# Gate products of a hybrid decoder layer in seven block products for eight

## The chip, the cores and the metric

The kernel runs on one core of a Trainium2 chip. The metric is the device time of one execution in microseconds (us); the median over the runs shown is what a change is measured by. The five engines are named as in the profile: PE (matrix products; PEld is its loading of weights), DVE (vector), ACT (scalar), POOL (GpSimd) and SP (which only issues transfers here).

## What is computed

One layer on 512 tokens of width 2048, float32. Only the part around the change is shown; the attention-like branch (`gated_delta_rule`), the pooling branch, the mixture of experts and the last gate lie before and behind it.

```python
n1 = rms_norm(h, norm_mix[i])                       # (512, 2048)
proj = n1 @ w_in[i]                                 # u_pool 1024, q, k, v, z 4096, b, a, then
u_pool, qkv, z, b_lin, a_lin, gate_pool, gate_dn = split_columns(proj)   # two gates of 2048
...
merged = (jax.nn.sigmoid(gate_pool) * (y_pool @ w_up_pool[i])
          + jax.nn.sigmoid(gate_dn) * (y_dn @ w_up_dn[i]))
h = h + merged @ w_out[i]
```

## The kernel before

Everything is held transposed: a tile has 128 channels on its partitions and the 512 tokens along the free axis. `n1h[k]`, `n1l[k]` (k = 0 to 15) hold the normed input as a rounded part and the rest, so that a float32 product is made of three products in the faster format, `mm3` (L99 to L103): high weights by high input, high weights by low input, low weights by high input. Each of the three is one matmul of 128x128 weights by 128x512 input.

Weights come in chunks of 128x1024 (`raw`, 512 KB): four k-tiles of 256 output columns. `load_w` (L324) has SP fetch a chunk and splits it: ACT rounds it into `whi` (L96), DVE subtracts to get `wlo` (L97, two inputs in SBUF, the on-chip memory of the engines). `next_w` hands out one chunk and starts the split of the next, so a split runs beside the matmuls of the chunk before it; `whi` and `wlo` have two buffers, `raw` three.

`proj` (L375) makes 256 output columns in two PSUM banks (PSUM is where PE accumulates): 24 matmuls for each chunk, four chunks for a gate (2048 channels in), two for an up-projection (1024 in). After the delta branch, whose last head ends at the start of this stage, `merge_dn` and `merge_pool` take eight column pairs each. For every pair `gate_up` makes the gate's product, ACT writes `sg` = tanh of half of it (a sigmoid is taken as (tanh + 1)/2), and then the up-projection's product is made from `ydh`, `ydl` or `yph`, `ypl`. DVE multiplies the two (L474, L486). In the first pair stands `pool_mix`, which needs the eight tiles `d` that `load_diffs` fetches from DRAM. The order of work on each engine here is that of a scheduler over the program's order.

Pools of SBUF are opened and closed like a stack, on a left and a right side; a tile in reused space waits until its predecessors there are done.

Of the kernel before, what the change touches and what calls it, by code (L numbers as in the profile page):

```python
# [21 lines left out]
KD = D // P  # L22
# [15 lines left out]
C_GP = 5136  # L38
C_GD = 7184
# [25 lines left out]
class Layer:  # L65
# [162 lines left out]
    def norm_in(self, sources):  # L228
        nc, px = self.nc, self.px
# [3 lines left out]
        self.rs = px.tile([P, NT], F32, name="rs", bufs=1)  # L233
        raw = []
        for _ in range(4):
            src, width = next(sources)
# [27 lines left out]
        ps = [self.bank("mm"), self.bank("mm")]  # L264
# [56 lines left out]
            self.xs.append(x)  # L321


    def load_w(self, src, width):  # L324
        nc = self.nc
        raw = self.p_w.tile([P, 1024], F32, name="raw", bufs=3)
        hi = self.p_w.tile([P, 1024], F32R, name="whi", bufs=2)
        lo = self.p_w.tile([P, 1024], F32R, name="wlo", bufs=2)
        r = raw.rearrange("p (k c) -> p k c", c=width)
        nc.sync.dma_start(r, src)  # L330
        self.last_split = self.split(hi, lo, raw)
        return hi.rearrange("p (k c) -> p k c", c=width), lo.rearrange("p (k c) -> p k c", c=width)

    def mixer_sources(self):
        a, w = self.a, self.a["w_in"][0]

        def cols(m, c0):
            for k0 in range(0, m.shape[0], 4 * P):
                yield m[k0:k0 + 4 * P, c0:c0 + 256].rearrange("(k p) c -> p k c", p=P), 256
# [4 lines left out]
        for c0, up in ((C_GD, a["w_up_dn"][0]), (C_GP, a["w_up_pool"][0])):  # L344
            for cp in range(8):
                yield from cols(w, c0 + cp * 256)
                yield from cols(up, cp * 256)
                if cp == 0 and c0 == C_GD:
                    for g in (0, 2):
                        yield a["pool_w"][0, g:g + 2].rearrange("g (k p) c -> p (g k) c", p=P), 256  # L350
        for cb in range(4):
            for k0 in range(0, KD, 2):
                yield a["w_out"][0, k0 * P:(k0 + 2) * P, cb * T:(cb + 1) * T].rearrange("(k p) c -> p k c", p=P), T

    def start_weights(self, sources):
        self.pending, self.side = [], iter(())
        self.w_sources = sources
        self.w_next = self.load_w(*next(sources))

    def next_w(self):  # L360

        w = self.w_next
        src = next(self.w_sources, None)
        self.w_next = src and self.load_w(*src)
        return w

    @contextmanager
# [4 lines left out]
                s.enter_context(self.tc.issue_after(i.ins))  # L372
            yield

    def proj(self, xh, xl, tag="mm"):  # L375

        nk = len(xh)
        ps = [self.bank(tag), self.bank(tag)]
        for k0 in range(0, nk, 4):
            hi, lo = self.next_w()  # L380
            for k in range(4):
                for c in range(2):
                    s = slice(c * P, (c + 1) * P)
                    self.mm3(ps[c], hi[:, k, s], lo[:, k, s], xh[k0 + k], xl[k0 + k],
                             start=k0 + k == 0, stop=k0 + k == nk - 1)
                with self.behind(self.last_split):
                    self.tick()
                    if k in EXTRA:
                        self.tick()
        return ps  # L390

    def tick(self):
        if self.pending:
            self.pending.pop(0)()
        else:
            next(self.side, None)
# [56 lines left out]
                    self.yph.append(h)  # L453
                    self.ypl.append(l)

    def gate_up(self, pp, yh, yl):

        nc = self.nc
        ps = self.proj(self.n1h, self.n1l)
        sg = []  # L460
        for i in range(2):
            s = pp.tile([P, T], F32, name="sg", bufs=3)
            nc.scalar.activation(s, ps[i], AF.Tanh, scale=0.5)
            sg.append(s)
        return sg, self.proj(yh, yl)

    def merge_dn(self, pp):
        for cp in range(8):
            sg, ps = self.gate_up(pp, self.ydh, self.ydl)
            for i in range(2):  # L470
                n = 2 * cp + i
                if n >= 8:
                    self.md.append(self.p_md.tile([P, T], F32, name="md", tag=f"md{n}", bufs=1))
                self.nc.vector.scalar_tensor_tensor(self.md[n], sg[i], 1.0, ps[i], op0=OP.add, op1=OP.mult)  # L474
            if cp == 0:
                self.pool_mix()

    def merge_pool(self, pp):

        nc = self.nc  # L480
        self.m = []
        for cp in range(8):
            sg, ps = self.gate_up(pp, self.yph, self.ypl)
            for i in range(2):
                t = self.p_y.tile([P, T], F32, name="m", tag="yd", bufs=KD)
                nc.vector.scalar_tensor_tensor(t, sg[i], 1.0, ps[i], op0=OP.add, op1=OP.mult)  # L486
                nc.vector.tensor_tensor(t, t, self.md[2 * cp + i], op=OP.add)
                self.m.append(t)

# [1195 lines left out]
    def run(self):  # L1685
# [9 lines left out]
        self.p_dram = p_dram = self.ctx.enter_context(tc.tile_pool(name="saved", bufs=1, space=bass.MemoryType.DRAM))  # L1695
        self.h_dram = p_dram.tile([T, D], F32, name="h_dram")
        self.d_dram = p_dram.tile([8, P, T], F32, name="d_dram")
        self.p_n1, s_n1 = self.open("n1", "right")
        with tc.manual_schedule(engines={mybir.EngineType.Activation, mybir.EngineType.DVE, mybir.EngineType.PE}):
            self.norm_in(self.mixer_sources())  # L1700
# [6 lines left out]
        self.delta_branch(pd)  # L1707
        s_d.close()
        s_dc.close()
        self.p_md, s_md = self.open("md", "left")  # L1710
# [6 lines left out]
        s_n1.close()  # L1717
        s_yp.close()
        s_md.close()
        p_h, s_h = self.open("hp", "right")  # L1720
# [6 lines left out]
        pp, s_p = self.open("out_tmp", "left")  # L1727
# [13 lines left out]
        pp, s_p = self.open("router_tmp", "right")  # L1741
# [10 lines left out]
        pp, s_p = self.open("tail", "left")  # L1752
# [41 lines left out]
```

## Time and profile before

| | |
|---|---|
| time, median of 3 runs | 2546.79 us (2546.7 to 2548.34) |
| the profiled execution's own time | 2548.15 us |
| its span in the trace | 2546.4 us |
| mean granted clock of PE in it | 0.989 of full |

The profile is that of one execution; its span is shorter than its own time by 1.75 us, which lie around the first and the last instruction. Its rows are those of the sections below. A matmul's duration in them (389 ns for 512 columns) is that from its start to its end, and consecutive matmuls overlap: what PE delivers is read from the distance of their starts, in the timeline.

### The profile page before, as it was taken

The numbers are of one execution on the slowest core, as the hardware profiler recorded it, in microseconds if no ns is written. First come the engines' busy times: TensorE is split into PE (matmuls) and PEld (weight loads), VectorE is DVE, ScalarE is ACT, GpSimd is POOL, SyncE is SP. The second block draws the span as 40 slices with busy tenths as digits, with TensorE's granted clock in tenths as the row PEclk, the third lists the DMA queues.
The fourth block names the chain that finished last, engine by engine and source line by source line (L and its number), as shares of the span: only waits on it lengthen the run. The fifth ranks groups of instructions, "written<-read, shape, count | busy, mean of one in ns | idle before, by whom it ended". The sixth has DMA issues, their size and how long they took to land. (4 is left out here: it accounts for less than half of the span.)

```text
span 2546.4 us, 30523 instructions
## 1 busy us (share of the span) xinstructions
PE 2411.1 (95%) x11926; PEld 1652.8 (65%) x11926; DVE 1063.4 (42%) x1963; ACT 719.8 (28%) x1323; POOL 83.6 (3%) x92
## 2 busy tenths in 40 slices
PE   7999999999999999999998978999989989987998
PEld 6788888888888888877774523533533433353888
DVE  6475757665422232334445412422423312324435
ACT  5233332423322222224445401400311300114323
POOL 1001011100000000000000000000000000000002
PEclk9999999999999999999998999999999999999999
DMA  5232222233233233247226799999999999998322
GB/s 158 76 88 67 76 72 81 67 97 124 91 99 99 92 99 98 93 155 275 90 88 235 290 386 421 420 421 421 420 421 421 420 380 421 419 419 304 116 83 100
DMA packets 201047, 554.13 MB, mean 218 GB/s; under 512 B 30377, under 2 KB 127042, under 8 KB 152130
## 3 DMA queue, kind: packets, MB, share of 16 engines
q1 hardware_dynamic: 197682, 543.61, 56.2%
q10 hardware_dynamic: 2640, 4.33, 0.5%
q0 software_dynamic: 576, 4.19, 0.4%
q8 instruction: 95, 1.56, 0.3%
q14 instruction: 54, 0.44, 0.0%
HBM read 545.01 MB, written 7.08 MB: 217 GB/s over the span
## 5 line engine op out<-in xcount | busy, mean ns | idle before, releaser
L1181 PE MATMUL ps_mm<-wm,xe 128*64 128x512 f32 (+1 forms) x2048 | 437.9, 607 | 46.5 <-DMA wm<-in_w_up_dram 28.6
L101 PE MATMUL ps_mm<-n1h,whi 128*128 128x512 f32 x1120 | 450.3, 402 | 0.9 <-ACT whi L96 0.9
L103 PE MATMUL ps_mm<-n1h,wlo 128*128 128x512 f32 x1120 | 437.3, 391 | 1.5 <-DVE wlo L97 1.4
L102 PE MATMUL ps_mm<-n1l,whi 128*128 128x512 f32 x1120 | 437.1, 390 | 0.0
L97 DVE TENSOR_TENSOR wlo<-raw,whi 128x1024 fp32r<-128x1024 f32 x206 | 254.5, 1235 | 408.9 <-ACT whi L96 401.1
L96 ACT CAST whi<-raw 128x1024 fp32r<-128x1024 f32 x206 | 216.3, 1050 | 545.1 <-PE ps_mm L102 544.2
L1181 PEld LDWEIGHTS ps_mm<-wm,xe 128*64 128x64 f32 (+1 forms) x2048 | 123.6, 128 | 322.7 <-issue 211.1
L1267 DVE TENSOR_TENSOR h<-h,ps_dl 128x512 f32<-128x512 f32 x208 | 130.2, 682 | 387.6 <-PE ps_dl L1265 387.6
L103 PEld LDWEIGHTS ps_mm<-n1h,wlo 128*128 128x128 f32 x1120 | 210.0, 188 | 47.2 <-DVE wlo L97 2.4
L101 PEld LDWEIGHTS ps_mm<-n1h,whi 128*128 128x128 f32 x1120 | 210.8, 188 | 40.3 <-ACT whi L96 1.3
L102 PEld LDWEIGHTS ps_mm<-n1l,whi 128*128 128x128 f32 x1120 | 210.9, 188 | 38.5
L1243 PE MATMUL ps_mm<-wm,hmT 128*64 128x512 f32 (+1 forms) x896 | 192.1, 610 | 16.7 <-DMA wm<-in_w_down_dram 7.4
L97 DVE TENSOR_TENSOR glo<-h,ghi 128x512 fp32r<-128x512 f32 x80 | 88.7, 1120 | 126.6 <-ACT ghi L96 126.2
L1243 PEld LDWEIGHTS ps_mm<-wm,hmT 128*64 128x64 f32 (+1 forms) x896 | 55.1, 131 | 123.1 <-issue 99.2
L96 ACT CAST ghi<-h 128x512 fp32r<-128x512 f32 x80 | 90.2, 1146 | 137.4 <-PE ps_dl L1161 97.4
L1161 PE MATMUL ps_dl<-G,ghi 128*128 128x384 f32 (+1 forms) x320 | 101.9, 332 | 1.0 <-DVE G L1131 1.0
L103 PE MATMUL ps_mm<-whi,ml 128*128 128x512 f32 x256 | 100.7, 393 | 2.1 <-DVE ml L97 2.1
L101 PE MATMUL ps_mm<-whi,mh 128*128 128x512 f32 x256 | 100.8, 394 | 0.0
L102 PE MATMUL ps_mm<-wlo,mh 128*128 128x512 f32 x256 | 100.7, 394 | 0.0
L1162 PE MATMUL ps_dl<-G,glo 128*128 128x384 f32 (+1 forms) x320 | 98.1, 320 | 1.0 <-DVE glo L97 1.0
L1227 ACT ACTIVATE yhi<-ps_mm,sc 128x512 fp32r<-128x512 f32 x52 | 35.7, 690 | 205.9 <-PE ps_dl L1264 113.6
L1228 DVE SCALAR_TENSOR_TENSOR ylo<-ps_mm,sc,yhi 128x512 fp32r<-128x512 f32 x52 | 39.0, 751 | 118.7 <-ACT yhi L1227 116.6
(417 smaller groups left out, 3292.3 us busy)
## 6 DMA issues: line engine op xcount, KB each, us to landing
wm<-in_w_gate_dram SPq DMA_DIRECT2D x128, 1024.0 KB, 18.9
wm<-in_w_up_dram SPq DMA_DIRECT2D x128, 1024.0 KB, 17.8
wm<-in_w_down_dram SPq DMA_DIRECT2D x128, 1024.0 KB, 19.8
raw<-in_w_in_dram SPq DMA_DIRECT2D x144, 512.0 KB, 3.5
raw<-in_w_out_dram SPq DMA_DIRECT2D x32, 512.0 KB, 3.6
wm<-in_w_ple_gate_dram SPq DMA_DIRECT2D x16, 1024.0 KB, 5.1
raw<-in_w_up_dn_dram SPq DMA_DIRECT2D x16, 512.0 KB, 3.5
raw<-in_w_up_pool_dram SPq DMA_DIRECT2D x16, 512.0 KB, 3.4
```

Source lines behind the costliest of these rows:

```text
L96: i = self.nc.scalar.copy(hi, src)
L97: return i, self.nc.vector.tensor_tensor(lo, src, hi.bitcast(F32), op=OP.subtract)
L101: mm(ps, whi, xhi, start=start, stop=False)
L102: mm(ps, whi, xlo, start=False, stop=False)
L103: mm(ps, wlo, xhi, start=False, stop=stop)
L1161: nc.tensor.matmul(p, hi[:, t, :], G[:, t, c0:c0 + n], start=t == 0, stop=False)
L1162: nc.tensor.matmul(p, lo[:, t, :], G[:, t, c0:c0 + n], start=False, stop=t == NT - 1)
L1181: nc.tensor.matmul(ps[w * i:w * i + w, :], xe[:, k, w * i:w * i + w], ws[i][:, j, :], start=k == 0, stop=k == KD - 1)
L1227: nc.scalar.activation(yh, ps, AF.Copy, scale=sc[:, 2:3])
L1228: nc.vector.scalar_tensor_tensor(yl, ps, sc[:, 2:3], yh.bitcast(F32), op0=OP.mult, op1=OP.subtract)
L1243: nc.tensor.matmul(out[cb][r, :], hT[:, k, r], ws[i][:, cb * T:(cb + 1) * T], start=k == 0, stop=k == 3)
L1267: nc.vector.tensor_tensor(d, d, pc, op=OP.add)
```

## The change

The gates of both branches (16 column pairs) are all made first, in `gates`, before any up-projection. Their tanh goes to DRAM (`g_dram`, 512 KB a pair, issued on ACT's queue) and comes back as `sg` for each up-projection on SP's queue (`gate`), one pair ahead. `n1` is closed after the gates, so that `sg`'s pool lies where it was.

The first pair is made as before, by `proj`; meanwhile `combine_x` forms, for each of eight pairs of k-tiles, the sums that Strassen's scheme (Winograd's form of it, with 7 products and 15 additions) wants of the input: the 2x2 blocks are two k-tiles by two halves of the tokens. DVE adds the high and low parts again (`full`), POOL makes four differences (`tsum`), ACT and DVE split them into `th`, `tl` and, in place, into the second half of `n1h[k]`, `n1l[k]`. The other 15 pairs go through `proj_seven`: each `raw` chunk is used in two halves (2 k-tiles by 256 columns, four blocks of 128x128), POOL makes four sums of blocks (`sums`), ACT and DVE split blocks and sums, and PE makes seven products of 128x128 weights by 128x256 input, three matmuls each, into seven half banks. After the eighth half one ACT copy and seven DVE additions combine the seven half banks into the pair's 256 columns, and ACT takes the tanh.

```diff
-    def load_w(self, src, width):
...
-        self.last_split = self.split(hi, lo, raw)
+    def split_weights(self, sources):
+        nc = self.nc
+        for src, width, seven in sources:
+            raw = self.p_w.tile([P, 1024], F32, name="raw", bufs=3)
+            nc.sync.dma_start(raw.rearrange("p (k c) -> p k c", c=width), src)
+            for j in range(2 if seven else 1):
+                hi = self.p_w.tile([P, 1024], F32R, name="whi", bufs=2)
+                lo = self.p_w.tile([P, 1024], F32R, name="wlo", bufs=2)
+                if not seven:
+                    self.last_split = self.split(hi, lo, raw)
+                    yield [x.rearrange("p (k c) -> p k c", c=width) for x in (hi, lo)]
+                    continue
+                a = raw[:, 512 * j:512 * j + 512]
+                a11, a21, a12, a22 = (a[:, P * i:P * i + P] for i in range(4))
+                sums = self.p_sums.tile([P, 4, P], F32, name="sums", bufs=2)
+                add = partial(nc.gpsimd.tensor_tensor, op=OP.add)
+                sub = partial(nc.gpsimd.tensor_tensor, op=OP.subtract)
+                add(sums[:, 0], a21, a22)
+                sub(sums[:, 1], sums[:, 0], a11)
+                sub(sums[:, 2], a11, a21)
+                sub(sums[:, 3], a12, sums[:, 1])
+                self.split(hi[:, 0:512], lo[:, 0:512], a)
+                self.split(hi[:, 512:], lo[:, 512:], sums.rearrange("p i c -> p (i c)"))
+                yield [x.rearrange("p (i c) -> p i c", c=P) for x in (hi, lo)]
...
+    def combine_x(self, k, xh, xl):
+        nc, h = self.nc, T // 2
+        f = self.p_c.tile([P, 2, T], F32, name="full", tag="c", bufs=4)
+        for i in range(2):
+            nc.vector.tensor_tensor(f[:, i], xh[k + i].bitcast(F32), xl[k + i].bitcast(F32), op=OP.add)
+        t = self.p_c.tile([P, 4, h], F32, name="tsum", tag="c", bufs=4)
+        sub = partial(nc.gpsimd.tensor_tensor, op=OP.subtract)
+        sub(t[:, 0], f[:, 0, h:], f[:, 0, 0:h])
+        sub(t[:, 1], f[:, 1, h:], t[:, 0])
+        sub(t[:, 2], f[:, 1, h:], f[:, 0, h:])
+        sub(t[:, 3], t[:, 1], f[:, 1, 0:h])
+        th = self.p_t.tile([P, 3, h], F32R, name="th", bufs=KD // 2)
+        tl = self.p_t.tile([P, 3, h], F32R, name="tl", bufs=KD // 2)
+        self.split(th, tl, t[:, 1:4])
+        self.split(xh[k][:, h:], xl[k][:, h:], t[:, 0])
...
+    def proj_seven(self, xs, tag):
+        nc, h = self.nc, T // 2
+        banks = [self.bank(tag) for _ in range(4)]
+        ps = [b[:, h * i:h * i + h] for b in banks for i in range(2)]
+        pairs = ((0, 0), (2, 1), (5, 4), (4, 3), (6, 5), (7, 2), (3, 6))
+        for j, x in enumerate(xs):
+            hi, lo = self.next_w()
+            for i, (a, b) in enumerate(pairs):
+                self.mm3(ps[i], hi[:, a], lo[:, a], *x[b], start=j == 0 and i % 2 == 0,
+                         stop=j == len(xs) - 1 and i in (1, 3, 5, 6))
+        p1, p2, p6, p5, p7, p3, p4 = ps[:7]
+        tt = nc.vector.tensor_tensor
+        e = self.p_c.tile([P, 4, h], F32, name="e", bufs=2)
+        c = self.p_c.tile([P, 2, T], F32, name="c", bufs=4)
+        nc.scalar.copy(e[:, 0], p1)
+        tt(c[:, 0, 0:h], e[:, 0], p2, op=OP.add)
...
+        tt(c[:, 1, 0:h], e[:, 3], p4, op=OP.subtract)
+        return c
...
+    def gates(self):
+        nc = self.nc
+        xs = []
+        def more(k0):
+            for k in (k0, k0 + 2):
+                xs.append(self.combine_x(k, self.n1h, self.n1l))
+        for n in range(16):
+            if n == 0:
+                ps = self.proj(self.n1h, self.n1l, after=more)
...
+            else:
+                c = self.proj_seven(xs, "dl" if n % 2 else "mm")
+                nc.scalar.activation(c, c, AF.Tanh, scale=0.5)
+            nc.scalar.dma_start(self.g_dram[n], c.rearrange("p i t -> p (i t)"))
+    def gate(self, pp, n):
+        if n < 16:
+            g = pp.tile([P, 2, T], F32, name="sg", bufs=3)
+            self.nc.sync.dma_start(g.rearrange("p i t -> p (i t)"), self.g_dram[n])
+            self.sg[n] = g
     def merge_dn(self, pp):
+        self.sg = {}
+        self.gate(pp, 0)
         for cp in range(8):
-            sg, ps = self.gate_up(pp, self.ydh, self.ydl)
+            self.gate(pp, cp + 1)
+            ps = self.proj(self.ydh, self.ydl)
...
+        self.p_c, s_c = self.open("combined", "left")
+        self.p_sums, s_su = self.open("sums", "left")
+        self.p_t, s_t = self.open("combined_x", "left")
+        self.gates()
...
```

PE's queue is that of before up to the end of the first gate pair and from the last up-projection on; ACT's and DVE's up to the delta branch's last `yd` and from the output projection on. In between they stand as follows; line numbers are those of the changed file where a row is of the change.

The first place is DVE's queue where the delta stage ends and the first gate pair runs. Before, behind the last head's `yd` (the delta branch's output), only splits of weight chunks (`wlo`), the splits of `d` and the first products `md` stand there:

```order
L97 TENSOR_TENSOR yd<-y,yd 128x512
L97 TENSOR_TENSOR wlo<-raw,whi 128x1024
L97 TENSOR_TENSOR d<-d,dh 128x512 x4
L97 TENSOR_TENSOR wlo<-raw,whi 128x1024 x4
L474 SCALAR_TENSOR_TENSOR md<-sg,ps_mm 128x512 x2
```

With the change the sums and splits of the input stand there; these rows are the end of that piece, with the splits for the halves 1 and 2 of the first `proj_seven`:

```order
L423 TENSOR_TENSOR full<-n1h_120,n1l_136 128x512
L423 TENSOR_TENSOR full<-n1h_121,n1l_137 128x512
L423 TENSOR_TENSOR full<-n1h_122,n1l_138 128x512
L97 TENSOR_TENSOR n1l_136<-tsum,n1h_120 128x256
L423 TENSOR_TENSOR full<-n1h_123,n1l_139 128x512
L97 TENSOR_TENSOR wlo<-raw,whi 128x512
L97 TENSOR_TENSOR tl<-tsum,th 128x768
L97 TENSOR_TENSOR n1l_138<-tsum,n1h_122 128x256
L97 TENSOR_TENSOR wlo<-sums,whi 128x512
L97 TENSOR_TENSOR tl<-tsum,th 128x768
L97 TENSOR_TENSOR wlo<-raw,whi 128x512
L97 TENSOR_TENSOR wlo<-sums,whi 128x512
```

The splits of half 1 stand among the last sums of the input, and those of half 2 (the last two rows) behind the last `tl` of all.

The second place is DVE's queue at the border of two gate pairs. Before, two products stand between the chunk splits of one pair and of the next:

```order
L97 TENSOR_TENSOR wlo<-raw,whi 128x1024 x6
L474 SCALAR_TENSOR_TENSOR md<-sg,ps_mm 128x512 x2
L97 TENSOR_TENSOR wlo<-raw,whi 128x1024 x6
L474 SCALAR_TENSOR_TENSOR md<-sg,ps_mm 128x512 x2
L97 TENSOR_TENSOR wlo<-raw,whi 128x1024 x6
```

With the change (the first two rows split half 0 of the next pair, the last two its half 1):

```order
L97 TENSOR_TENSOR wlo<-raw,whi 128x512
L97 TENSOR_TENSOR wlo<-sums,whi 128x512
L454 TENSOR_TENSOR c<-e,ps_dl 128x256
L455 TENSOR_TENSOR e<-e,ps_dl 128x256
L456 TENSOR_TENSOR e<-e,ps_dl 128x256
L457 TENSOR_TENSOR e<-e,ps_dl 128x256
L458 TENSOR_TENSOR c<-e,ps_dl 128x256
L459 TENSOR_TENSOR c<-e,ps_dl 128x256
L460 TENSOR_TENSOR c<-e,ps_dl 128x256
L97 TENSOR_TENSOR wlo<-raw,whi 128x512
L97 TENSOR_TENSOR wlo<-sums,whi 128x512
```

Seven additions out of PSUM have come between the splits of half 0 and half 1.

The third place is POOL's queue. Before, it has nothing between the last head (`vr`) and the router. With the change the differences of the input and the sums of the weights stand there, 32 and 480 instructions; a piece near the end of the input's:

```order
L346 TENSOR_TENSOR sums<-raw,sums 128x128
L426 TENSOR_TENSOR tsum<-full 128x256
L427 TENSOR_TENSOR tsum<-full,tsum 128x256
L428 TENSOR_TENSOR tsum<-full 128x256
L429 TENSOR_TENSOR tsum<-tsum,full 128x256
L343 TENSOR_TENSOR sums<-raw 128x128
L345 TENSOR_TENSOR sums<-raw 128x128
L344 TENSOR_TENSOR sums<-sums,raw 128x128
L346 TENSOR_TENSOR sums<-raw,sums 128x128
```

From there on, four instructions of 128x128 stand there for each half of a chunk.

## Rows read from the trace of the kernel before

**Rows 1.** The page: busy us, share of span, instructions

```profile
PE 2411.1 (95%) x11926; PEld 1652.8 (65%) x11926; DVE 1063.4 (42%) x1963; ACT 719.8 (28%) x1323; POOL 83.6 (3%) x92
```

**Rows 2.** Gate stage: us, busy of PE, PEld, DVE, ACT, POOL; clock, DMA

```profile
608.50:1143.10 534.60, 533.63 (x2355) 441.21 (x2354) 161.82 (x165) 129.27 (x148) 0.00 (x0) 1.00 0.33 105
```

**Rows 3.** PE groups of that stage: busy us, mean ns, idle before

```profile
L101 PE MATMUL ps_mm<-n1h,whi 128*128 128x512 f32 x512 | 199.4, 389 | 0.9 <-ACT whi L96 0.9
```

**Rows 4.** Timeline of PE in a gate product: start us, us

```profile
699.94 0.39 PE L101 MATMUL ps_mm<-n1h,whi 128*128 128x512 f32 x1
...
702.66 0.39 PE L101 MATMUL ps_mm<-n1h,whi 128*128 128x512 f32 x1
```

**Rows 5.** Timeline of PE in the first product, 256 columns at a time

```profile
45.89 0.28 PE L101 MATMUL ps_mm<-n1h,fhi 128*128 128x256 f32 x1
...
49.01 0.28 PE L103 MATMUL ps_mm<-n1h,flo 128*128 128x256 f32 x1
```

**Rows 6.** Timeline of PE in the last products of the tail

```profile
2509.86 0.28 PE L102 MATMUL ps_dl<-wlo,xh 128*128 128x256 f32 x1
...
2512.89 0.28 PE L101 MATMUL ps_dl<-whi,xh 128*128 128x256 f32 x1
```

**Rows 7.** Whole span, groups by shape on ACT and DVE

```profile
L96 ACT CAST mh<-m 128x512 fp32r<-128x512 f32 x64 | 39.7, 622 | 102.7 <-PE ps_mm L102 102.7
L97 DVE TENSOR_TENSOR ml<-m,mh 128x512 fp32r<-128x512 f32 x64 | 44.2, 692 | 81.5 <-ACT mh L96 78.2 <-PE ps_mm L103 1.6 <-PE ps_mm L102 1.6
L1641 DVE SCALAR_TENSOR_TENSOR h<-th,h 128x256 f32<-128x256 f32 x8 | 3.2, 421 | 0.1
```

**Rows 8.** Timeline of DVE and POOL near the start

```profile
25.98 0.20 POOL L91 TENSOR_TENSOR rsq_b<-rsq_b,ms 128x2 f32<-128x2 f32 x1
26.48 1.23 DVE L97 TENSOR_TENSOR flo<-raw,fhi 128x1024 fp32r<-128x1024 f32 x1
26.54 1.22 POOL L93 TENSOR_TENSOR rsq_j<-rsq_j,rsq_b 128x2 f32<-128x2 f32 x1
```

**Rows 9.** Timeline of DVE and POOL in the delta stage

```profile
202.93 1.23 DVE L97 TENSOR_TENSOR wlo<-raw,whi 128x1024 fp32r<-128x1024 f32 x1 [5.20 <-ACT whi L96]
203.07 3.00 POOL L636 TENSOR_TENSOR gm<-upper,glo 128x512 fp32r<-128x512 f32 x2 [52.86 <-PE ps_dl L766]
204.07 1.28 DVE L768 TENSOR_TENSOR pm<-ps_dl,lev 128x512 f32<-128x512 f32 x2
```

**Rows 10.** Timeline of DVE and POOL in the tail

```profile
2402.23 1.22 DVE L97 TENSOR_TENSOR wlo<-wm,whi 128x1024 fp32r<-128x1024 f32 x1
2402.84 3.46 POOL L1644 TENSOR_TENSOR h<-h,gain 128x512 f32<-128x512 f32 x2 [1073.24 <-ACT sqj L1643]
2403.37 1.78 DVE L1638 SCALAR_TENSOR_TENSOR th<-th,pj 128x512 f32<-128x512 f32 x1
2405.19 1.67 DVE L1641 SCALAR_TENSOR_TENSOR h<-th,h 128x512 f32<-128x512 f32 x1
```

**Rows 11.** Timeline of POOL, additions and products that nothing delays

```profile
507.77 1.28 POOL L687 TENSOR_TENSOR bd<-B,diag 128x512 f32<-128x512 f32 x1 [0.49 <-DVE B L684]
509.01 1.30 POOL L713 TENSOR_TENSOR E<-E,upper 128x512 f32<-128x512 f32 x1
2521.03 0.73 POOL L1644 TENSOR_TENSOR h<-h,gain 128x256 f32<-128x256 f32 x1 [1.42 <-ACT sqj L1643]
```

**Rows 12.** Timeline where the delta stage ends

```profile
608.50 0.48 PE L101 MATMUL ps_mm<-n1h,whi 128*128 128x512 f32 x1
612.17 0.69 DVE L97 TENSOR_TENSOR yd<-y,yd 128x512 fp32r<-128x512 f32 x1 [0.69 <-ACT yd L96]
```

**Rows 13.** DMA issues of the gate stage: KB each, median us to landing

```profile
d<-d_dram SPq DMA_DIRECT2D x8, 256.0 KB, 5.2
```

**Rows 14.** Granted clock (PEclk) around PE's idle time in the router

```profile
1344.00:1356.00 12.00, 1.54 (x16) 0.81 (x14) 9.30 (x48) 3.17 (x6) 0.00 (x0) 0.67 0.34 124
1356.00:1361.80 5.80, 5.55 (x24) 5.28 (x25) 4.38 (x10) 3.27 (x6) 0.00 (x0) 0.50 0.00 0
```

More of the change, by code (lines that the diff above doesn't have):

```diff
@@ L235, in norm_in @@
         for _ in range(4):
-            src, width = next(sources)
+            src = next(sources)[0]
             w = self.p_w.tile([P, 4, 256], F32, name="raw", bufs=3)
@@ L343, in mixer_sources @@
                 yield from cols(w, COLS[kind] + n * 256)
-        for c0, up in ((C_GD, a["w_up_dn"][0]), (C_GP, a["w_up_pool"][0])):
+        for i, c0 in enumerate((C_GD, C_GP)):
             for cp in range(8):
-                yield from cols(w, c0 + cp * 256)
+                yield from cols(w, c0 + cp * 256, i + cp > 0)
+        for i, up in enumerate((a["w_up_dn"][0], a["w_up_pool"][0])):
+            for cp in range(8):
                 yield from cols(up, cp * 256)
-                if cp == 0 and c0 == C_GD:
+                if i + cp == 0:
                     for g in (0, 2):
-                        yield a["pool_w"][0, g:g + 2].rearrange("g (k p) c -> p (g k) c", p=P), 256
+                        yield a["pool_w"][0, g:g + 2].rearrange("g (k p) c -> p (g k) c", p=P), 256, False
         for cb in range(4):
             for k0 in range(0, KD, 2):
-                yield a["w_out"][0, k0 * P:(k0 + 2) * P, cb * T:(cb + 1) * T].rearrange("(k p) c -> p k c", p=P), T
+                yield a["w_out"][0, k0 * P:(k0 + 2) * P, cb * T:(cb + 1) * T].rearrange("(k p) c -> p k c", p=P), T, False
     def start_weights(self, sources):
         self.pending, self.side = [], iter(())
-        self.w_sources = sources
-        self.w_next = self.load_w(*next(sources))
+        self.w_stream = self.split_weights(sources)
+        self.w_next = next(self.w_stream)
     def next_w(self):
         w = self.w_next
-        src = next(self.w_sources, None)
-        self.w_next = src and self.load_w(*src)
+        self.w_next = next(self.w_stream, None)
         return w
@@ L373, in behind, with proj @@
             yield
-    def proj(self, xh, xl, tag="mm"):
+    def proj(self, xh, xl, tag="mm", after=None):
         nk = len(xh)
@@ L389, in proj @@
                         self.tick()
-        return ps
+            if after:
+                after(k0)
+        return ps
+    def combine_x(self, k, xh, xl):
[13 more added lines that the diff above has]
+        self.split(xh[k][:, h:], xl[k][:, h:], t[:, 0])
+        return [(a[:, 0:h], b[:, 0:h]) for a, b in ((xh[k], xl[k]), (xh[k + 1], xl[k + 1]))] + [
+            (xh[k + 1][:, h:], xl[k + 1][:, h:]), (xh[k][:, h:], xl[k][:, h:]),
+            *((th[:, i], tl[:, i]) for i in range(3))]
+    def proj_seven(self, xs, tag):
[14 more added lines that the diff above has]
+        tt(c[:, 0, 0:h], e[:, 0], p2, op=OP.add)
+        tt(e[:, 1], e[:, 0], p6, op=OP.add)
+        tt(e[:, 2], e[:, 1], p5, op=OP.add)
+        tt(e[:, 3], e[:, 1], p7, op=OP.add)
+        tt(c[:, 1, h:], e[:, 2], p7, op=OP.add)
+        tt(c[:, 0, h:], e[:, 2], p3, op=OP.add)
+        tt(c[:, 1, 0:h], e[:, 3], p4, op=OP.subtract)
+        return c
     def tick(self):
@@ L482, in merge_pool @@
         for cp in range(8):
-            sg, ps = self.gate_up(pp, self.yph, self.ypl)
+            self.gate(pp, cp + 9)
+            ps = self.proj(self.yph, self.ypl)
             for i in range(2):
                 t = self.p_y.tile([P, T], F32, name="m", tag="yd", bufs=KD)
-                nc.vector.scalar_tensor_tensor(t, sg[i], 1.0, ps[i], op0=OP.add, op1=OP.mult)
+                nc.vector.scalar_tensor_tensor(t, self.sg[8 + cp][:, i], 1.0, ps[i], op0=OP.add, op1=OP.mult)
                 nc.vector.tensor_tensor(t, t, self.md[2 * cp + i], op=OP.add)
```

29 lines of the change are left out of this document (11 added, 18 removed).

## The prediction

> **What bounds it now.** I read the busy shares first, then the stages, then single rows of the stage that the change touches. PE is busy 95% of the span [rows 1]. The stage from the first gate matmul to the output projection takes 534.6 us; PE fills it and does not wait, at the full clock (1.00, that is 2.4 GHz), while DVE is busy 161.8 us of it, ACT 129.3 and POOL not at all [rows 2, 3]. So this stage is worth what its matmuls are worth, as long as the other three keep up. The duration of a matmul (389 ns) is no price, since the next one starts before it ends: twelve matmuls of 512 columns start within 2.72 us, **0.2267 us each** [rows 4]. The stage's 2352 matmuls (1536 for gates, 768 up, 48 in `pool_mix`) times 0.2267 are 533 us: that is the stage.
>
> **The matmuls removed.** A gate pair has 96 matmuls of 512 columns, 21.76 us. The change has 168 of 256 columns (8 halves of 21). The trace has 256-column matmuls with the same operands in the same roles, weights that change every time and a half of `n1h` as input: 26 start within 3.12 us, **0.120 us each** [rows 5]. In the tail, 26 start within 3.03 us, 0.1165 [rows 6]; half of the 512-column pitch would be 0.1133. I take rows 5, whose operands are those of the change: 168 x 0.120 = 20.16 us a pair, 2.52 us a half. Fifteen pairs: **-24 us** (bounds -33 by rows 6, -41 by half the pitch). The larger number of weight loads costs no more than is in that pitch.
>
> The Trainium skill's page "TensorE: Matmul & The Clock Gate", section "Back-to-back issue gap", gives an isolated gap of columns / 2.4 + 2.5 ns; from that I estimate 20.7 us against 18.4 us a pair, -35 us in all. The trace is above the page at both widths (0.2267 against 0.216, 0.120 against 0.109), so the rows stand.
>
> **POOL and DVE in one another's way.** The change gives POOL 512 instructions in a stage where it had none, and they run beside DVE's splits. What that does is seen in three places. A POOL product of 2 elements, 0.20 us otherwise, took 1.22 us: it started just after a DVE split of `flo` and ended 0.05 us after it [rows 8]. In the tail, POOL's product waits for `wlo` to end, DVE's next instruction with two SBUF inputs takes 1.78 us where its like takes 0.69 and ends at 2405.15; POOL's second product ends 1.15 us after that, at 2406.30, and DVE's following one, 1.67 us long, 0.56 us after that [rows 10, 7]. So a DVE instruction with two SBUF inputs and a POOL one take turns, whole instruction by whole instruction. DVE's with PSUM as one input do not: two `pm` took their normal 1.28 us while POOL ran [rows 9]. The splits `wlo` and the additions `full` are of the first kind; the seven additions behind a pair are of the second.
>
> The Trainium skill says it as a rule: "SBUF — State Buffer", section "SBUF: two separate sides", has DVE and GpSimd share one port pair under an exclusive lock, held for a whole instruction, against DVE instructions with two SBUF inputs too. The trace agrees (rows 8 and 10). Without the rule, reading busy shares alone, one would forecast the gain of the matmuls, about 2523 us.
>
> Prices of a turn, from rows: DVE holds for 0.56 us at 512 columns [rows 10], so, less the same 0.13 us of start, 0.82 at 768, 0.29 at 256, 1.1 at 1024. POOL holds 1.15 us of the 1.30 it takes at 512 columns; at 256 it takes 0.73 us alone, so about 0.58 held [rows 10, 11]. At **128 columns the trace has no row**: between 0.20 us (2 columns) and 0.73 us (256) a straight line gives 0.46 us, of which 0.31 held; back to back 0.03 less, 0.43 [rows 8, 11].
>
> **Steady state.** In each half of 2.52 us POOL has four 128-column sums and DVE two splits of 512. The turns alone add up to 4 x 0.31 + 2 x 0.56 = 2.36 us, just under 2.52. But POOL's four take 4 x 0.43 + 0.08 (the last waits for the third) = 1.8 us by themselves, and DVE's two turns push into that: 1.8 + 1.12, less some 0.24 that falls into POOL's pauses, is 2.68, 0.16 over. With no overlap it is 1.8 + 2 x 0.69 = 3.2. At the border of pairs DVE's queue has the splits of half 0, seven additions (0.42 each alone [rows 7], 2.5 us overlapped) and then the splits of half 1. Half 0's buffer is free only when half 7 starts, 2.52 us ahead of the border; cast, two `wlo`, seven additions and one more `wlo` end 2.8 us after the border, when PE wants them at 2.76. Without POOL that fits; each wait of up to 0.31 us for POOL is then PE's, three or four a border, about 1.2 us. The two delays are not added, since PE's pause lets POOL catch up: I take **1.35 us a pair, +19 us** for 14 pairs (bounds 0 and 0.68 x 8 x 14 = +76).
>
> **The first two pairs.** The sums of the input start when DVE has the last `yd` behind it, at 612.86, 4.4 us after the first gate matmul [rows 12]. Turns up to the last `tl`: 16 `full` x 0.56, 32 POOL differences x 0.58, 8 x (0.82 + 0.29) of splits, two chunk splits x 1.1, and for halves 0 to 2 twelve sums x 0.31 and four `wlo` x 0.56: 45 us, so not before 657.5. Half 2's `wlo` stands behind that `tl` in DVE's queue, and six halves are then left, 15.1 us: pair 1 ends at 673, where matmuls alone would have it at 608.5 + 21.8 + 20.2 = 650.5. That is 22 us late. The input's sums share a ring of four buffers (two chains in flight), and the chunk casts stand behind these chains in ACT's queue, so the port will not be used without gaps: I take **+30 us** (bounds: +7 if nothing took turns, POOL's 27.6 us alone; +38 if the chains run one after another).
>
> PE then has pauses of several us. Behind an idle PE the trace shows the clock at 0.50, 1.2 GHz: 5.8 us of matmuls ran at half clock after the router [rows 14], 2.9 us lost. One or two such: **+4 us** (0 to 12).
>
> **Other moves.** Each up-projection of 10.9 us needs one `sg`, fetched one pair ahead, and two chunks: 1.5 MB in 10.9 us beside 105 GB/s now [rows 2]; hidden. If it were not, each would cost its landing, 16 x 3.5. The tiles `d` were fetched beside the first gate; now SP issues them behind the last gate, and three `sg` and chunks stand in front. They landed in 5.2 us each [rows 13], the first up-projection gives 10.9 us of cover: **+2 us** (0 to 8). The tanh (ACT) and the store lie beside the next pair.
>
> **Sum.** -24 + 19 + 30 + 4 + 2 = +31 us on 2548.15 of the profiled execution, or 2546.79 + 31 = **2578 us** against the median.
>
> **Rivals.**
> 1. *The turns cost little; the gain of the matmuls comes through.* If 128-column sums on POOL take 0.35 us or less, the four fit beside the splits, borders cost nothing, and the input's sums cost 12 us: -24 + 12 + 2 = -10, 2537 us. For it: 2.36 < 2.52. Against: rows 8 and 10, and the input's 45 us of turns. It decides in favour of the change where the first two pairs lose under 20 us and a half takes 2.52. Chance 0.12.
> 2. *POOL becomes the bound outright.* No overlap of starts and turns, 3.2 us a half: -24 + 76 + 38 + 6 = +96, 2643 us. For it: POOL's pauses between its instructions were 0.03 us, little for DVE to slip into. Against: in rows 10 they alternate cleanly. Chance 0.14.
> 3. *The parts cancel.* POOL at 0.40 us gives no steady loss beyond the border's 0.3 us a pair and the first pairs lose 18: about 0, 2547 us. Chance 0.08.
>
> **Numbers.** My forecast, a loss of 6 to 75 us with delays in both places, has 0.66. About 0.2% (5 us) is what a measurement tells from no change. Faster 0.12 (rival 1), same 0.08 (rival 3), slower 0.80. The forecast's own cases go from 2553 to 2622; the range takes in half of rival 3's and most of rival 2's, 2547 to 2640, and leaves out rival 1 and some 0.08 more.
>
> **What would show it.** The pitch of 256-column matmuls at 0.120. POOL sums of 0.46 us when alone, longer beside `wlo`; `wlo` of 512 columns above 0.69. A steady pair of about 21.5 us with a wait of PE for `wlo` in half 1; the first `proj_seven` twice as long as a later one. The step is wrong if PE waits for nothing after pair 1, if pairs take over 23 us (POOL's price), or if the store or `sg` appears as a releaser.

## The result

The changed kernel takes 2580.97 us in the median (2579.08 to 2582.32), against 2546.74 us for the kernel before on the same chip: a ratio of 1.0134, 95% interval 1.0116 to 1.0151. The forecast was 2578.

The page of the changed kernel's profiled execution (span 2579.6 us) begins with the busy times, as in [rows 1]:

```profile
PE 2406.8 (93%) x13006; PEld 1694.6 (66%) x13006; DVE 1241.9 (48%) x2280; ACT 814.3 (32%) x1519; POOL 410.3 (16%) x604
```

PE's busy time hardly changes, though it has 1080 instructions more; POOL's is five times as long. The stage that answers to [rows 2], its first two pairs and a stretch of steady pairs, with the same columns:

```profile
608.50:1172.20 563.70, 525.46 (x3431) 482.01 (x3429) 343.61 (x486) 224.80 (x345) 326.55 (x512) 0.97 0.41 126
608.50:681.20 72.70, 52.41 (x264) 46.04 (x263) 49.00 (x57) 23.75 (x41) 56.13 (x72) 0.77 0.19 58
700.00:960.00 260.00, 247.72 (x2037) 245.22 (x2036) 180.40 (x278) 132.59 (x219) 237.69 (x389) 1.00 0.42 124
```

The stage is 29 us longer, and PE, which was idle for 1 us of it, stands idle for 38 us. 20.3 of them lie in the first two pairs, where the mean granted clock is 0.77 (0.50, that is 1.2 GHz, from 650 to 665 us, 1.00 again from 675 us), and 12.3 in the 260 us of steady pairs, at full clock. POOL is busy 91% of the steady stretch. The matmuls themselves came out as priced from [rows 5]; 26 start within 3.12 us:

```profile
799.79 0.28 PE L102 MATMUL ps_dl<-tl,whi 128*128 128x256 f32 x1
...
802.91 0.28 PE L101 MATMUL ps_dl<-th,whi 128*128 128x256 f32 x1
```

What PE waits for, by releaser, from the first gate matmul to a little past the stage (us in total, times, longest):

```profile
PE ps_dl L103 <- DVE wlo L97: 19.3, 12, 4.5
PE ps_mm L103 <- DVE wlo L97: 11.8, 7, 5.6
PE ps_mm L101 <- ACT mh L96: 3.5, 1, 3.5
PE ps_mm L101 <- ACT whi L96: 3.4, 2, 2.5
PE ps_dl L102 <- DVE d L97: 0.2, 1, 0.2
```

31 us are waits for a late `wlo`. When each pair was done is read from ACT's tanh, which starts 2.3 us after the last matmul of pair 1 and 3.2 us after that of a steady pair. First those of pairs 0 (two instructions) and 1, then two in the steady stretch:

```profile
658.34 0.59 ACT L541 ACTIVATE c<-ps_mm 128x512 f32<-128x512 f32 x1
662.17 0.59 ACT L541 ACTIVATE c<-ps_mm 128x512 f32<-128x512 f32 x1
683.53 1.06 ACT L544 ACTIVATE c<-c 128x1024 f32<-128x1024 f32 x1 [1.22 <-DVE c L460]
...
747.91 1.06 ACT L544 ACTIVATE c<-c 128x1024 f32<-128x1024 f32 x1 [0.96 <-DVE c L460]
769.40 1.06 ACT L544 ACTIVATE c<-c 128x1024 f32<-128x1024 f32 x1 [0.96 <-DVE c L460]
```

Pair 1 ends at about 681.2 (683.53 less 2.3), against 650.5 for the bare matmuls: 30.7 us late, slow clock included. A steady pair takes 21.49 us, against 20.16 for its matmuls. PE's pause in a steady pair is one wait, at the first matmul of half 1 that needs the late `wlo`:

```profile
770.19 0.38 PE L103 MATMUL ps_mm<-n1h,wlo 128*128 128x256 f32 x1 [1.03 <-DVE wlo L97]
```

Beside it, POOL's weight sums and DVE's splits in one half:

```profile
762.92 0.46 POOL L343 TENSOR_TENSOR sums<-raw 128x128 f32<-128x128 f32 x1
763.34 0.46 POOL L345 TENSOR_TENSOR sums<-raw 128x128 f32<-128x128 f32 x1
763.65 0.70 DVE L97 TENSOR_TENSOR wlo<-sums,whi 128x512 fp32r<-128x512 f32 x1 [1.01 <-ACT whi L96]
763.76 0.91 POOL L344 TENSOR_TENSOR sums<-sums,raw 128x128 f32<-128x128 f32 x1
764.27 0.94 DVE L97 TENSOR_TENSOR wlo<-raw,whi 128x512 fp32r<-128x512 f32 x1
764.75 0.79 POOL L346 TENSOR_TENSOR sums<-raw,sums 128x128 f32<-128x128 f32 x1
765.50 0.46 POOL L343 TENSOR_TENSOR sums<-raw 128x128 f32<-128x128 f32 x1
```

The first two sums run alone, 0.46 us each and 0.42 apart. The third starts 0.11 us after a split and ends 0.32 after it (764.67 against 764.35), the fourth 0.33 after the next split: they take turns. From one L343 to the next it is 0.42 + 0.42 + 0.99 + 0.75 = **2.58 us, where the half's matmuls take 2.52**.

That distance is not the same in all eight halves of a pair. From 746.25 to 767.75 us it is 3.06, 2.70, 2.70, 3.04, 2.58, 2.58, 2.58 and 2.25 us, together the pair's 21.49. The first of them holds the only pause of POOL in the pair. Here is that pause two pairs later, with the last of the seven additions and the splits ahead of it:

```profile
790.43 0.41 DVE L460 TENSOR_TENSOR c<-e,ps_mm 128x256 f32<-128x256 f32 x1
790.76 0.84 DVE L97 TENSOR_TENSOR wlo<-raw,whi 128x512 fp32r<-128x512 f32 x1
791.53 0.68 DVE L97 TENSOR_TENSOR wlo<-sums,whi 128x512 fp32r<-128x512 f32 x1
792.28 0.46 POOL L343 TENSOR_TENSOR sums<-raw 128x128 f32<-128x128 f32 x1 [1.23 <-DVE wlo L97]
```

`sums` has two buffers. The split that reads one of them stands on DVE's queue behind the additions, and POOL cannot begin the next sums until it is done. So POOL loses 1.23 us at each border of the steady stretch.

The third loss lies behind the gates, where the output projection begins:

```profile
1169.49 2.00 ACTq L975 DMA_DIRECT2D h<-in_x_dram  x4
1171.54 1.66 ACT L96 CAST mh<-m 128x512 fp32r<-128x512 f32 x3 [1.95 <-DVE m L578]
...
1172.21 0.80 PE L101 MATMUL ps_mm<-whi,mh 128*128 128x512 f32 x1 [3.47 <-ACT mh L96]
```

ACT issues four loads of x into `h` only here, and the casts `mh` stand behind them on ACT's queue, with PE waiting 3.47 us. The kernel before waits 2.1 us at this place, for `ml`, so 1.4 us are new. At 1204.47 us, within the output projection, PE waits 3.39 us more, for `whi`. The landings of `d`, 5.2 us in [rows 13], are little changed, and no wait of PE is for `sg` or the store:

```profile
g_dram<-c ACTq DMA_DIRECT2D x16, 512.0 KB, 5.3
...
sg<-g_dram SPq DMA_DIRECT2D x16, 512.0 KB, 3.7
...
d<-d_dram SPq DMA_DIRECT2D x8, 256.0 KB, 6.1
```

### The profile page after: what moved, and what is told of

It is laid out like the page before. It is cut to its first block, busy times and chain, and to the rows that moved or that the text cites. A ratio compares the mean times of both kernels' runs of the same rounds, so it can differ in the third digit from the quotient of the medians.

```text
span 2579.6 us, 33974 instructions
## 1 busy us (share of the span) xinstructions
PE 2406.8 (93%) x13006; PEld 1694.6 (66%) x13006; DVE 1241.9 (48%) x2280; ACT 814.3 (32%) x1519; POOL 410.3 (16%) x604
## 5 line engine op out<-in xcount | busy, mean ns | idle before, releaser
L97 DVE TENSOR_TENSOR wlo<-raw,whi 128x1024 fp32r<-128x1024 f32 (+1 forms) x266 | 285.8, 1074 | 191.8 <-ACT whi L96 178.0
L96 ACT CAST whi<-raw 128x1024 fp32r<-128x1024 f32 (+1 forms) x266 | 227.4, 855 | 403.8 <-PE ps_mm L102 356.1
L101 PE MATMUL ps_mm<-n1h,whi 128*128 128x512 f32 (+1 forms) x864 | 327.7, 380 | 2.5 <-ACT whi L96 2.5
L103 PE MATMUL ps_mm<-n1h,wlo 128*128 128x512 f32 (+1 forms) x864 | 315.7, 366 | 13.3 <-DVE wlo L97 13.3
L102 PE MATMUL ps_mm<-n1l,whi 128*128 128x512 f32 (+1 forms) x864 | 314.4, 364 | 0.0
L103 PEld LDWEIGHTS ps_mm<-n1h,wlo 128*128 128x128 f32 x864 | 163.6, 189 | 41.8 <-DVE wlo L97 15.6
L101 PEld LDWEIGHTS ps_mm<-n1h,whi 128*128 128x128 f32 x864 | 164.4, 190 | 23.3 <-ACT whi L96 2.9
L102 PEld LDWEIGHTS ps_mm<-n1l,whi 128*128 128x128 f32 x864 | 164.4, 190 | 20.1
L97 DVE TENSOR_TENSOR wlo<-sums,whi 128x512 fp32r<-128x512 f32 x120 | 90.0, 750 | 60.1 <-ACT whi L96 56.3
L96 ACT CAST whi<-sums 128x512 fp32r<-128x512 f32 x120 | 74.4, 620 | 92.7 <-POOL sums L346 92.5
```

The lines of the kernel that those rows point to most:

```text
L96: i = self.nc.scalar.copy(hi, src)
L97: return i, self.nc.vector.tensor_tensor(lo, src, hi.bitcast(F32), op=OP.subtract)
L101: mm(ps, whi, xhi, start=start, stop=False)
L102: mm(ps, whi, xlo, start=False, stop=False)
L103: mm(ps, wlo, xhi, start=False, stop=stop)
```

## The experiments

Twelve kernels ran, each beside the kernel before on its chip. The table gives the time, the ratio to the kernel before with its 95% interval, and the distance of the tanh of two steady pairs. Three kernels leave work out, which sends wrong numbers into the later stages, so that their total says nothing.

| kernel | us | ratio | steady pair, us |
|---|---|---|---|
| the change | 2580.97 | 1.0134 (1.0116 to 1.0151) | 21.48 |
| e1_no_sums | not read | | 20.16 |
| e2_ahead2 | 2576.63 | 1.0109 (1.0094 to 1.0125) | 21.24 |
| e3_plain3 | 2562.16 | 1.0054 (1.0040 to 1.0068) | 21.47 |
| e4_order | 2557.71 | 1.0035 (1.0022 to 1.0049) | 21.76 |
| e5_dve_sums | 2562.02 | 1.0055 (1.0042 to 1.0068) | 20.23 |
| e6_n1_late | 2553.43 | 1.0018 (1.0009 to 1.0027) | 21.76 |
| e7_x_on_dve | 2571.64 | 1.0095 (1.0080 to 1.0109) | 21.48 |
| e8_best | 2546.17 | 0.9992 (0.9983 to 1.0000) | 20.23 |
| e9_mix_later | 2545.70 | 0.9984 (0.9975 to 0.9993) | 20.23 |
| e10_x_too | 2538.34 | 0.9955 (0.9942 to 0.9969) | 20.23 |
| e11_no_additions | not read | | 21.11 |
| e12_tanh_only | not read | | 20.83 |

The kernel before stood at 2548.53 us beside e1 to e4, at 2548.33 beside e5 to e8, at 2548.78 beside e9 to e11.

**Where a steady pair loses its 1.3 us: e1, e2, e5, e11, e12.** First the weight sums away:

```diff
-                add(sums[:, 0], a21, a22)
...
-                sub(sums[:, 3], a12, sums[:, 1])
-                self.split(hi[:, 512:], lo[:, 512:], sums.rearrange("p i c -> p (i c)"))
+                self.split(hi[:, 512:], lo[:, 512:], a)
```

> Leaves out the four sums of weight blocks on POOL (600 operations become 120 fewer sets of four) and splits the loaded half-block a second time in their place; everything else stands. If the forecast's mechanism holds, that POOL's turns at the lock it shares with DVE stretch each split and so the splits behind the seven additions come late, the wait of about 1.3 us at the third matmul of half 1 shrinks to under 0.5 us, a steady pair takes 20.2 to 20.7 us in place of 21.48, the first pairs end a little earlier too, and the time is 2558 to 2568 us. The rival, that the order of the seven additions ahead of the split on DVE's queue costs this by itself, keeps the pair at 21.3 to 21.5 us and the time at 2576 to 2582 us.

The pair falls to the bare matmuls, 20.16 us, further than expected, and PE does not pause for 260 us:

```profile
700.00:960.00 260.00, 260.00 (x2156) 259.43 (x2155) 163.31 (x296) 133.78 (x230) 0.00 (x0) 1.00 0.45 135
```

The seven additions ahead of the split were still there, so they alone cost nothing; the rival is out. The total that was expected can't be read. The tanh of pair 1 also starts 7.15 us earlier (676.38).

The second experiment gives the splits a longer lead:

```diff
+                third = seven and u % 3 == 0
+                pool = self.p_sums if third else self.p_w
+                hi = pool.tile([P, 1024], F32R, name="whi", bufs=1 if third else 2)
...
+        while len(self.w_ready) < self.w_ahead:
+            self.w_ready.append(next(self.w_stream, None))
```

> All is computed; the splits of the gate stage run two halves ahead in three buffers in place of one half ahead in two (the scratch of the additions is cut to make room). If the border wait comes from one late split behind seven additions while each half alone fits (turns of 2.36 us in a half of 2.52), a second half of lead covers the 1.3 us: pairs of 20.2 to 20.4 us, no wait of PE for wlo after pair 3, 2560 to 2567 us. If POOL or DVE is in truth full over a whole pair (the rival in which POOL is the bound), lead cannot help: pairs of 21.2 us or more, 2574 to 2582 us.

The pair only goes from 21.48 to 21.24 us: my expectation failed, and its rival's numbers held. It does not prove the rival, that the cycle is too long whatever the lead. The edit gives a third buffer to `whi` and `wlo` and none to `sums`, and POOL's pause at the border is as long as before, 1.23 us in each pair. A third buffer of `sums` was not tried. The next one takes the turns away but keeps the work:

```diff
-                add = partial(nc.gpsimd.tensor_tensor, op=OP.add)
-                sub = partial(nc.gpsimd.tensor_tensor, op=OP.subtract)
+                add = partial(nc.vector.tensor_tensor, op=OP.add)
+                sub = partial(nc.vector.tensor_tensor, op=OP.subtract)
```

> All is computed; the four sums of weight blocks are made by DVE in place of POOL. Without the sums a pair took 20.16 us, the bare matmuls, and with two halves of lead 21.24 us, so what is full is the turns of POOL and DVE over a whole pair (about 2.3 us a half and 2.9 us of additions), not the place of the additions on the queue. On DVE alone a half is two splits of 0.69 us and four sums of about 0.2 us, 2.2 us, and a pair with its additions 20.5 us: pairs of 20.2 to 20.9 us and, with 2547 us for the kernel before, 2562 to 2573 us. The rival, that DVE's own work is what is full and each sum moved to it adds to it, gives pairs of 22 us or more and 2588 us or more.

The groups of DVE in the same stretch, by shape (busy us, mean ns):

```profile
L97 DVE TENSOR_TENSOR wlo<-raw,whi 128x512 fp32r<-128x512 f32 x103 | 70.8, 688 | 12.8 <-ACT whi L96 12.1
...
L346 DVE TENSOR_TENSOR sums<-raw,sums 128x128 f32<-128x128 f32 x102 | 29.4, 288 | 1.7
```

A sum takes 0.29 us on DVE, a split of blocks again 0.69 (0.87 in the changed kernel), and the pair 20.23 us with DVE busy 243.4 of 260 us. More work on one engine is faster here than less work on two that exclude each other.

Whether POOL's cycle or the additions fill the pair was then asked from the other side, by leaving the additions out:

```diff
-        tt(c[:, 0, 0:h], e[:, 0], p2, op=OP.add)
...
-        tt(c[:, 1, 0:h], e[:, 3], p4, op=OP.subtract)
+        for i in range(2):
+            nc.scalar.copy(c[:, i], banks[i])
```

> Leaves out the combination of the seven products: ACT copies the first two banks into c, and what follows works on wrong gates, so that only the gate stage is read, not the time. If POOL's and DVE's turns for the splits (about 2.3 us a half, 18.4 us a pair) and the additions (2.9 us) together overfill a pair of 20.16 us, the pair takes 20.16 to 20.3 us without the additions though POOL's sums stay. If the turns alone are longer than a half of 2.52 us, the pair stays at 21 us or more.

The pair stayed at 21.05 to 21.12 us, so the first branch, mine, fell. But the edit gave ACT 0.7 us more at the border: in its timeline the two copies and the tanh run from 765.67 to 767.83, the split of the next half starts at 768.38, and POOL still pauses, 0.63 us a pair. The last run takes the tanh straight from PSUM instead (the edit against e11):

```diff
-            nc.scalar.copy(c[:, i], banks[i])
+            nc.scalar.activation(c[:, i], banks[i], AF.Tanh, scale=0.5)
...
-                nc.scalar.activation(c, c, AF.Tanh, scale=0.5)
```

> Leaves out the combination of the seven products and reads tanh from the first two banks, so that DVE has no additions and ACT has less to do at the border of two pairs than in the changed kernel (two tanh of about 0.6 us from PSUM); what follows works on wrong gates, so only the gate stage is read. In the runs so far POOL's last sum of a half comes every 2.58 us, above the 2.52 us of the matmuls: two splits that hold the memory 0.56 us each, two sums behind them at 0.31 us and two sums in a row at 0.42 us. If this cycle is the bound by itself, a pair takes 8 times 2.58, 20.5 to 20.8 us. If the cycle is absorbed by the lead and only the additions lose time, 20.16 to 20.3 us. If the border's work on ACT is what delays the splits (as e11_no_additions could have it, with 21.1 us), 21 us or more.

The pair takes 20.83 us, a hair above the first branch, and its stretch shows who is full:

```profile
700.00:960.00 260.00, 257.60 (x2098) 253.73 (x2097) 154.59 (x200) 134.71 (x226) 252.25 (x400) 1.00 0.42 128
```

POOL is busy 97% with the additions gone, and in no steady pair does it pause for more than 0.08 us: its sums, in turns with DVE's splits, fill the pair. So the weight sums without the additions cost a pair 0.67 us (20.83 less 20.16, e12), the additions without the sums nothing (e1), and both together 1.32. The 0.65 between e12 and the change are what the two do to one another (e12 also spares ACT one copy a pair), and the change's trace shows how: POOL's pause behind the additions, which e12 does not have.

**The first pairs: e3, e7.** Three pairs by eight products, the input's sums spread over them:

```diff
+            if n < 2:
+                xs.append(self.combine_x(8 * n + k0 // 2, self.n1h, self.n1l))
+                return
+            for k in (k0, k0 + 2):
+                self.replace_x(k, self.n1h, self.n1l)
...
-            if n == 0:
+            if n < 3:
```

> All is computed; three pairs go by eight products in place of one, the sums of inputs are spread over the first two and the half that they overwrite is replaced in the third. If the loss of about 31 us in the first pairs is the crowd of input sums and their turns, then of it 24 to 30 us go and two pairs at 21.76 in place of about 21.4 cost under 1 us: 2551 to 2559 us. If instead starting with seven products costs it wherever it begins (clock, first weight sums), the loss moves along: 2575 to 2583 us.

The gate stage ends 20.25 us earlier (its last tanh at 962.99 in place of 983.24); pairs 0 and 1 still have 5.6 us of waits. The result is 3 us above the expected range: the gain was 20, not 24 to 30. The loss did not move along, so most of it belongs to the crowd in the first pairs. The other edit leaves the place and changes the engine (`nc.gpsimd` to `nc.vector` in `combine_x`):

> All is computed; of the change only the four input sums of each pair of blocks go from POOL to DVE. If the loss in the first pairs is turns, as forecast (45 us of turns in pair 0), about 34 us of DVE work and the splits of the weights stay and the first two pairs end 8 to 12 us earlier: 2568 to 2574 us with 2547 us for the kernel before. If it is DVE's own time, the longer DVE work eats the gain: 2578 to 2586 us.

The tanh of pair 1 starts at 674.28, 9.25 us earlier, within the expected 8 to 12: about a third of the loss goes when POOL has no part in the input's sums. DVE makes them in 0.45 us each, 32 of them, and up to the end of pair 1 is busy only 51.8 us, against 49.0 in the change, since its other instructions take less time: `full` 0.72 us for 0.91, a split of 1024 columns 1.22 for 1.57.

**The order: e4, e6.** Only the new order and the way through DRAM, with eight products throughout:

```diff
-                yield from cols(w, c0 + cp * 256, i + cp > 0)
+                yield from cols(w, c0 + cp * 256, False)
...
-            if n == 0:
+            if n < 16:
```

> All is computed, by eight products throughout: only the order (all gates first) and the way of tanh through DRAM stay of the change. If the waits of the output projection's first matmuls (3.5 us for mh, 3.4 us for whi) and those in the up-projections belong to the order, the time is 2551 to 2558 us, against 2546.8 of the kernel before. If they come from what the seven products leave behind, it is 2545 to 2549 us.

It costs 9.2 us (2557.71 against 2548.53), and the same two waits stand in the output projection:

```profile
1145.06 2.01 ACTq L975 DMA_DIRECT2D h<-in_x_dram  x4
1147.78 0.50 PE L101 MATMUL ps_mm<-whi,mh 128*128 128x512 f32 x1 [3.48 <-ACT mh L96]
...
1180.47 0.80 PE L101 MATMUL ps_mm<-whi,mh 128*128 128x512 f32 x1 [3.28 <-ACT whi L96]
```

The change gives `n1`'s memory back before the merges, so the tiles `sg` lie where `h` comes to lie later, and the loads of `h` must wait for the last product of the merge. In the kernel before they start from 1132.6 us on, ahead of the output projection. From 1165 to 1182 us of e4 the DMA engines are busy all the time (a share of 1.02 by the view), and the `whi` of 1180.47 waits for its chunk to land. One moved line tells whether that is it:

```diff
         s_c.close()
-        s_n1.close()
...
         s_s.close()
+        s_n1.close()
```

> All is computed by eight products in the new order, as in e4_order; the one edit is that the memory of n1 is given back after the merges, as in the kernel before, so that the tiles of the gates lie beyond it and the tile h of the output projection no longer falls on them. If the 9 us of the order come from that place (the four loads of x into h wait on ACT's queue for the last product of the merge, mh and the expert weights behind them shift), the waits for mh (3.5 us) and whi (3.3 us) go and the time is 2547 to 2551 us with 2547 us for the kernel before. If they come from the order itself or from the way through DRAM, it stays at 2554 to 2558 us.

Nearly half of it: 2553.43 us, 4.3 less. The wait for `whi` is gone. That for `mh` is 1.4 us, with 0.9 for `ml` behind it, about the 2.1 us of the kernel before. So both came from the place. But the loads of `h` now run at 957 to 975, together with those of `d`, and `pool_mix` waits 2.8 us for `dh`. Neither of the two branches had this.

**Put together: e8, e9, e10.** e8_best is e3, e5 and e6 in one:

> All is computed; three pairs by eight products with the input sums spread over them (e3_plain3), the weight sums on DVE (e5_dve_sums) and the memory of n1 given back after the merges (e6_n1_late). If the three terms are separate and each is what the single edits make it, the time is 2562 less 13 pairs at about 0.9 us and less about 7 us: 2539 to 2547 us with 2547 us for the kernel before, at or under it. If DVE is full in the seven-product pairs, or the wait of the output projection has another cause, it stays at 2553 us or more.

At 2546.17 us it is where the kernel before is, at the upper end of the expected range. The gate stage gave a little more than was expected (its last tanh at 950.05, 12.9 us before that of e3, where 13 pairs at 0.9 us were reckoned), but the collision behind it grew. The timeline of PE, and the landings around it (KB each, median us):

```profile
964.70 1.22 PE L101 MATMUL ps_dl<-dh,whi 128*128 128x512 f32 x2 [5.97 <-ACT dh L96]
```

```profile
h<-in_x_dram ACTq DMA_DIRECT2D x4, 1024.0 KB, 7.7
...
d<-d_dram SPq DMA_DIRECT2D x8, 256.0 KB, 10.1
```

So the mix was moved by two pairs:

```diff
-            if cp == 0:
+            if cp == 2:
                 self.pool_mix()
```

> All is computed; as e8_best, with the mix of the pooled differences two pairs later in the up-projections (the third pair in place of the first). In e8_best the four loads of x into h, 1024 KB each, now start at the gates' end, together with the eight loads of d, and PE waits 6.0 us for dh and then runs at half clock for about 10 us. If that collision is the price, the wait and the slow stretch go: 5 to 9 us less than e8_best, 2537 to 2542 us with 2547 to 2548 us for the kernel before, under it. If the wait only moves to another tile (sg, which the same loads delay), the time stays at 2544 us or more.

It stayed at 2545.70 us. The wait for `dh` is gone, and PE waits for the next weights in its place, whose cast on ACT waited 10.65 us for a landing: the second branch.

```profile
979.72 0.79 PE L101 MATMUL ps_mm<-yd,whi 128*128 128x512 f32 x1 [4.20 <-ACT whi L96]
```

Last, the input's sums on DVE as well (the edit of e7 on top of e9):

> All is computed; as e9_mix_later, with the input sums on DVE too. In e8_best the first two pairs still hold 6 to 7 us of waits of PE for wlo and half-clocked matmuls, with POOL's input sums beside them. If these waits are turns, 2 to 6 us go, against e9_mix_later. If DVE's longer work makes up for them, the two are within 1.5 us.

It took 7.4 us off, more than expected. Pairs 0 and 1 now end as in e4, which has no sums at all (tanh of pair 1 at 653.23 and 652.50), and no wait for `wlo` is left in the whole stage:

```profile
PE ps_mm L101 <- ACT whi L96: 5.2, 2, 4.2
PE ps_mm L101 <- ACT mh L96: 1.4, 1, 1.4
PE ps_dl L685 <- POOL vr L934: 1.2, 1, 1.2
PE ps_mm L103 <- DVE ml L97: 0.9, 1, 0.9
```

With 2538.34 us against 2548.78, **e10_x_too beats both kernels**, the one before by 0.45% (0.31 to 0.58).

## Why the prediction was right

The total was off by 3 us, and the direction and both main places were right. That it came so close is in part luck. Measured, the terms are -24, +17.5 for the steady state, +30.7 for the first pairs and +9.2 for the other moves, +33.4 in all: the first pairs were taken 3 us too high and the other moves 7 us too low. The size of the steady state was right with its parts wrong.

- **Matmuls, -24.** Right: 0.120 us apart, 20.16 us a pair bare, as e1 shows.
- **Turns of POOL and DVE.** The mechanism is shown: e1 (no sums) and e5 (sums on DVE) end the loss, e5 all but 0.07 us a pair, with everything else in place. So are the prices read from [rows 8, 10, 11]: 0.46 us for a sum alone, 0.32 us from a split's end to that of the sum behind it. The Trainium skill's page "SBUF — State Buffer", section "SBUF: two separate sides", has these two engines share a lock that is held for a whole instruction; the runs agree with it, e5 most plainly (a split back at 0.69 us).
- **Steady state, +19.** The size was right (1.32 us a pair, 17.5 us for the 14, since pair 2 takes only 20.52), the composition wrong. The step "The two delays are not added, since PE's pause lets POOL catch up" failed. It took about the larger of two: 0.16 us a half for the turns, 1.28 a pair, and 1.2 a border for the additions beside POOL. Measured, the turns alone cost 0.67 a pair (e12) and the additions alone nothing (e1, as the forecast had it), and together they cost 1.32, more than the sum of the two. POOL does not catch up at the border: it stands still there itself, 1.23 us, behind the split that the additions hold up. The forecast did not count the two buffers of `sums`. PE's wait stood where it was forecast, at the border.
- **First pairs, +30 and +4 for the clock.** Together 30.7, but differently split: PE was busy 52.4 of the 72.7 us, where the two pairs take 41.9 at full clock. So 20 are waits, and some 10 are matmuls at half clock, more than the 4 of the forecast. The last `tl` started at 662.30, after the bound of 657.5. e3, e7 and e10 show that it is the crowd: spreading it takes 20 us, taking POOL out of the input's sums takes 9, and both together, with the weight sums on DVE too, take all of it. The lower bound does not come out as written: 27.6 us from 612.86 and 15.1 of matmuls end pair 1 some 5 us late, not 7. Nothing else rests on it.
- **Other moves, +2.** This was mis-sized: it is 9.2 us by e4. The forecast looked at the loads that the change adds (`sg`, `d`, the store), which cost next to nothing, and not at where the new tiles lie. That the four loads of `h` on ACT's queue would wait for the tiles `sg` to be read was nowhere in it.
- **Rivals.** Rival 1 needed first pairs that lose under 20 us and a half of 2.52; they lose 30.7, and a steady pair takes an eighth of 21.48, 2.69, a half. Rival 2 had the right engine, as POOL's sums alone, in turns with the splits, overfill the pair (e12), but its price of 3.2 us a half was too high: DVE's starts and POOL's do overlap. Rival 3's sum of parts is excluded by the same rows.

What stays open is what a third buffer of `sums` would give: the trace shows that POOL's pause stands behind the additions, but no run takes the pause away and leaves the additions on DVE's queue and the sums on POOL. Nor was it tried by itself why the weights' load was late in e4 before 1180.47. The loads of `h` and of the expert weights beside it are the candidate, not shown: in the changed kernel the four loads of `h` land in 13.5 us (6.5 in the kernel before) and the expert weights in 17.2 and 19.1 (8.3 and 9.7). In e6, where `h` comes earlier, these weights land in 7.6 and 9.1 us again.

## What to carry to other kernels

An idle engine is no free capacity when its instructions exclude those of a busy one: price the pair of them as one engine, cycle by cycle, including the stretches that one of them runs alone. Two delays that each fit, or nearly fit, can cost more together, where one stops the engine that the other has no time to spare on: look for the ring of buffers that couples them. A longer lead is a lead only if every tile of the chain has the buffers for it. When a change moves where tiles live, ask of each tile which later transfer will land on its memory and what stands behind that transfer's issue on its queue.

## What the runs showed of the hardware that had not been expected

The same 128x128 sum takes 0.46 us on POOL when it is alone and 0.29 us on DVE. Beside DVE's splits POOL's third sum took 0.91 us and its fourth 0.79. So four sums moved onto the engine that was to be relieved made its own splits faster (those of blocks take a mean of 0.87 us in the changed kernel and 0.69 in e5, those of sums 0.74 and 0.69), and DVE busy 94% held PE up less than DVE and POOL at 69% and 91%.
